# Stick-breaking / S5 hybrid block: order of the projection's passes by quarter, and two small steps on other engines

## The chip, the core and the metric

One core of a Trainium2 chip runs the whole program. TensorE multiplies 128x128 stationary tiles with streams of up to 512 columns, VectorE (DVE), ScalarE (ACT) and GpSimd (POOL) work on tiles of 128 partitions in SBUF, and only the first two also read PSUM, where TensorE writes. SyncE (SP) issues the DMAs. Every engine takes its instructions strictly in order. The metric is the device time of one execution in microseconds.

## What is computed

One residual block over 2048 frames of width 1024, float32. The part that the change touches is the combined projection (columns q, k, v, u, 512 each), the norm of each head of q and k, and the recurrence of the S5 half.

```python
xn = rmsnorm(h, norm1_g)
proj = xn @ w_in
q, k, v, u = jnp.split(proj, [512, 1024, 1536], axis=-1)
qh = rmsnorm(heads(q), q_norm_g)      # 8 heads of 64
kh = rmsnorm(heads(k), k_norm_g)
sb = stick_breaking_attention(qh, kh, heads(v))   # causal over 2048 frames
ssm = s5_glu(u, ...)                  # complex diagonal recurrence, GELU, half-GLU
h = h + concat(rmsnorm(sb), rmsnorm(ssm)) @ w_out
h = h + relu(rmsnorm(h) @ w1) ** 2 @ w2
```

## The kernel before

Products are made from float32 pairs: each operand is split into a rounded high part and the remainder (`hi` on ACT, `lo` on DVE), and `mm3` (lines 89 to 92) issues three matmuls, high by high, high by low and low by high.

**Projection** (`proj_stream`). The 2048 frames are four quarters Q = 3, 2, 1, 0 of four tiles j of 128 frames. The weight matrix is four groups gi of 512 columns: 0 is q, 1 is k, 2 is v, 3 is u. A job is one tile times one group: 8 row blocks by 3 matmuls, 24 matmuls. The list `jobs` holds 16 u jobs first, then for each quarter 4 jobs each of k, q and v, 64 in all. Before a group begins, its 8 blocks are loaded (`load_w`, 256 KB each, four buffers `wr`) and split (`split_w`: one 128x512 copy on ACT at line 157, one 128x512 instruction on DVE at line 158) during the job ahead; nine buffers hold split blocks. So each quarter loads and splits the k, q and v weights anew: 13 groups, 104 blocks.

**Evacuation** (`evac`). A v tile is split into `v` (lines 259 and 260). A q or k tile is copied to `p` (line 269), squared (271), reduced to 8 sums on DVE (273), divided by 64 and given its epsilon on DVE (274), raised to -1/2 and multiplied in on POOL (275, 276). Four jobs later `fin` transposes it on TensorE (284), splits it into `hi` and `lo` (288, 289; one buffer each) and stores both. A closing flag `kv{Q}` lets the attention of that quarter start.

**SSM** (`ssm_stream`). Runs between the projection's jobs in 16 chains. A chain rotates the projected input (`X`), scans it on DVE (line 769), rotates it back, and feeds TensorE (794) with the result. The rotation back makes `t1 = Xr*EC` on POOL and `t2`, in which the two halves of 64 partitions change places, by two DVE products of 64x512 (lines 775 and 776), and then subtracts.

**What sets the order.** `build` runs the projection with the SSM until the SSM ends, then with the attention until the projection ends, then the attention with the mixing of quarter 3 (`mix_stream`) and its MLP, and so on. From the instructions that come out of this interleaving a scheduler lays down each engine's final queue ahead of time; at run time nothing is reordered.

Of the kernel before, what the change touches and what calls it, by code (L numbers as in the profile page):

```python
# [11 lines left out]
ALU = mybir.AluOpType  # L12
ACTF = mybir.ActivationFunctionType
# [7 lines left out]
HD = 64  # L21
# [41 lines left out]
class Kern:  # L63
# [12 lines left out]
    def tt(self, eng, out, a, b, op):  # L76
        eng.tensor_tensor(out=out, in0=a, in1=b, op=op)  # L77
# [57 lines left out]
    def proj_stream(self):  # L135
        nc, A, S = self.nc, self.A, self.S
        NW = 4
        U, KV = 3, [1, 0, 2]
        jobs = [(("u",), Q, j, U) for Q in (3, 2, 1, 0) for j in range(4)]
        for Q in (3, 2, 1, 0):  # L140
            for gi in KV:
                jobs += [((Q, gi), Q, j, gi) for j in range(4)]
        group = {jb[0]: jb[3] for jb in jobs}
        first = jobs[0][0]
        xneed = [i for i, jb in enumerate(jobs) if jb[3] in (U, KV[0])]
        wt, wraw, xraw, xs = {}, {}, {}, {}

        def load_w(s, k):
# [72 lines left out]
        for i, (s, Q, j, gi) in enumerate(jobs):  # L221
            last = i + 1 == len(jobs) or jobs[i + 1][0] != s
            nxt = jobs[i + 1][0] if last and i + 1 < len(jobs) else None
            if i + 2 < len(jobs) and jobs[i + 1][0] == s and jobs[i + 2][0] != s:
                for k in range(NW):
                    load_w(jobs[i + 2][0], k)
            if i:
                feed_x(i)
            ps = self.ps_m.tile([128, 512], F32, tag="m", name="m")
            x, st = xs[Q, j], self.xst[:, 4 * Q + j, :]  # L230
            for k in range(8):
                w = wt[s, k]
                self.mm3(ps, x[:, 0, k, :], x[:, 1, k, :], w[:, 0, :], w[:, 1, :], k == 0, k == 7)
                if nxt:
                    split_w(nxt, k)
                    if k + NW < 8:
                        load_w(nxt, k + NW)
                if k == 0 and gi == U:
                    if i == 0:
                        feed_x(i)  # L240
                    stats(Q, j)
                if k == 1:
                    while pend and pend[0][0] <= i:
                        pend.pop(0)[1]()
                if k % 2 == 1:
                    yield 1.3
            self.evac(Q, gi, j, ps, st, i)
            if j == 3 and gi in (U, 2):
                pend.append((i + 1, lambda f=f"{'u' if gi == U else 'kv'}{Q}": self.flags.add(f)))
        for _, f in pend:  # L250
            f()
# [1 line left out]
    def evac(self, Q, gi, j, ps, st, i):  # L253
        nc, S = self.nc, self.S
# [12 lines left out]
        else:  # L267
            p = self.p_p.tile([128, 8, 64], F32, tag="p", name="p")
            nc.scalar.activation(out=p.rearrange("p h d -> p (h d)"), in_=ps, func=ACTF.Copy)
            sq = self.p_sq.tile([128, 8, 64], F32, tag="sq", name="sq")  # L270
            nc.scalar.activation(out=sq, in_=p, func=ACTF.Square)
            ss = self.p_tiny.tile([128, 16], F32, tag="ss", name="ss")
            nc.vector.tensor_reduce(out=ss[:, 0:8], in_=sq, axis=AX.X, op=ALU.add)
            self.ts(nc.vector, ss[:, 0:8], ss[:, 0:8], 1.0 / HD, ALU.mult, st[:, 2:3], ALU.add)
            self.tt(nc.gpsimd, ss[:, 8:16], ss[:, 0:8], self.mhalf[:, 0:8], ALU.pow)
            self.tt(nc.gpsimd, p, p, ss[:, 8:16].unsqueeze(2).to_broadcast([128, 8, 64]), ALU.mult)
            dst = S["qS"] if gi == 0 else S["kS"]
# [342 lines left out]
    def ssm_stream(self):  # L620
# [3 lines left out]
        tt, ts = self.tt, self.ts  # L624
# [110 lines left out]
        def chain(st, q, half):  # L735
# [35 lines left out]
                    data1=Xr[:, i, :], initial=0.0 if half else cy[:, i, 3:4], op0=ALU.mult, op1=ALU.add)  # L771
            t1, t2 = T([128, 4, 128]), T([128, 4, 128])
            tt(pool, t1, Xr, EC, ALU.mult)
            tt(dve, t2[0:64], Xr[64:128], E2[64:128], ALU.mult)
            tt(dve, t2[64:128], Xr[0:64], E2[0:64], ALU.mult)
            tt(pool, Xr, t1, t2, ALU.subtract)
            if half == 1:
                nc.vector.memset(X[:, :, 0:1], 0.0)
                nc.vector.tensor_copy(out=cy[:, :, 0:1], in_=X[:, :, 128:129])
# [762 lines left out]
```

## Time and profile before

| | us |
|---|---|
| median of 3 runs | 2605.67 (2601.1 to 2611.37) |
| the profiled execution | 2611.11 |
| its span, first to last instruction | 2609.4 |
| TensorE, matmul busy | 2471.2 (95%) |
| VectorE busy | 2069.8 (79%) |
| ScalarE busy | 1360.0 (52%) |
| GpSimd busy | 1023.4 (39%) |
| mean granted TensorE clock | 0.973 |

Busy shares over the whole span hide that the program has stages with different limits. By the records of lines 91 and 816, the projection's matmuls run to 564 us and the SSM's last result tile is written at 433 us; the attention begins between these two. The rows further below are read by stage.

### The profile page before, as it was taken

What the parts mean: (1) busy time and instruction counts of PE and PEld (TensorE: products, weight loads), DVE (VectorE), ACT (ScalarE), POOL (GpSimd) and SP (SyncE); (2) the same over time, 40 slices, a digit from 0 to 9 for tenths busy, and PEclk for the clock granted to TensorE, in tenths of its full rate; (3) what the DMA queues carried; (4) which work ended last, traced back from release to release, by engine and by line L of the source; (5) the groups of instructions that cost most, each with busy time, mean ns of one, the idle gap of its engine ahead of it and who ended that gap; (6) DMA issues with size and microseconds to landing.
All of it is one profiled execution on the core that took longest, in us unless ns stands there. A gap on an engine that the chain in (4) does not pass through costs nothing.

```text
span 2609.4 us, 36346 instructions
## 1 busy us (share of the span) xinstructions
PE 2471.2 (95%) x11984; PEld 2030.9 (78%) x11984; DVE 2069.8 (79%) x2990; ACT 1360.0 (52%) x2481; POOL 1023.4 (39%) x922
## 2 busy tenths in 40 slices
PE   8898888998889999999899899999999999989999
PEld 6776677876768888888777688888877888868887
DVE  7699997888998888899988976676687666676764
ACT  6444444765666666666566644444334444434443
POOL 5685856866775445444556421122100000020010
PEclk9999999998999999999989899999999999999999
DMA  8635457773433434333424234555444443594564
GB/s 290 200 115 171 130 158 213 212 222 117 136 113 122 126 116 120 105 109 99 144 83 152 85 113 160 178 178 182 141 149 151 161 141 138 181 322 156 192 223 164
DMA packets 290221, 408.88 MB, mean 157 GB/s; under 512 B 28016, under 2 KB 157808, under 8 KB 289520
## 3 DMA queue, kind: packets, MB, share of 16 engines
q1 hardware_dynamic: 290032, 406.55, 48.5%
q8 instruction: 95, 1.56, 0.2%
q14 instruction: 94, 0.77, 0.1%
HBM read 321.39 MB, written 83.89 MB: 155 GB/s over the span
## 4 chain that ended last, share of the span: by engine, by line
PE 63%; DVE 6%; DMA 3%; issue 2%; ACT 1%; POOL 0%; SPq 0%; DVEq 0%; ACTq 0%; POOLq 0%
PE m L90 10%; PE m L92 10%; PE m L91 10%; PE g L91 3%; PE g L92 3%; PE z L353 3%; PE g L90 3%; PE at L393 3%; PE o L413 2%; PE o L412 2%; PE fy L90 2%; PE fy L91 2%; PE fy L92 2%; DVE C L377 1%; DMA w<-in_w_dram 1%
## 5 line engine op out<-in xcount | busy, mean ns | idle before, releaser
L77 POOL TENSOR_TENSOR a<-a,C 128x512 f32<-128x512 f32 (+1 forms) x320 | 464.9, 1463 | 363.7 <-DVE C L377 134.2
L90 PE MATMUL m<-h,w 128*128 128x512 f32 (+1 forms) x992 | 359.2, 365 | 5.1 <-DVE h L77 2.7
L92 PE MATMUL m<-h,w 128*128 128x512 f32 (+1 forms) x992 | 357.8, 362 | 5.5 <-DVE w L77 5.4
L91 PE MATMUL m<-h,w 128*128 128x512 f32 (+1 forms) x992 | 357.7, 362 | 2.0 <-DVE h L77 1.9
L377 DVE TENSOR_TENSOR_SCAN C<-s,C,mz 128x513 f32<-128x513 f32 x192 | 273.4, 1440 | 16.7 <-ACT s L368 7.7
L368 ACT ACTIVATE s<-z 128x512 f32<-128x512 f32 (+1 forms) x320 | 172.2, 539 | 155.7 <-PE z L353 149.1
L397 ACT ACTIVATE hi<-at 128x512 fp32r<-128x512 f32 (+1 forms) x320 | 170.1, 541 | 140.5 <-PE at L393 123.8
L91 PE MATMUL m<-w,x 128*128 128x512 f32 x512 | 210.9, 412 | 14.7 <-DVE w L158 14.5
L77 DVE TENSOR_TENSOR lo<-at,hi 128x512 fp32r<-128x512 f32 (+1 forms) x320 | 185.7, 595 | 48.5 <-ACT hi L397 47.0
L90 PE MATMUL m<-w,x 128*128 128x512 f32 x512 | 208.9, 411 | 14.8 <-DVE v L260 6.1
L90 PEld LDWEIGHTS m<-h,w 128*128 128x128 f32 x992 | 189.3, 191 | 34.9 <-ACT w L909 3.0
L92 PEld LDWEIGHTS m<-h,w 128*128 128x128 f32 x992 | 189.4, 191 | 34.3 <-DVE w L77 7.6
L91 PEld LDWEIGHTS m<-h,w 128*128 128x128 f32 x992 | 189.8, 192 | 29.7 <-DVE h L77 4.0
L77 DVE TENSOR_TENSOR h<-h,m 128x512 f32<-128x512 f32 x256 | 170.1, 675 | 50.6 <-PE m L92 50.3
L92 PE MATMUL m<-w,x 128*128 128x512 f32 x512 | 208.3, 407 | 0.5 <-DVE x L77 0.5
L90 PE MATMUL m<-a,w 128*128 128x512 f32 x512 | 202.4, 396 | 2.2 <-DVE h L77 2.1
L91 PE MATMUL m<-a,w 128*128 128x512 f32 x512 | 200.4, 392 | 0.0
L92 PE MATMUL m<-a,w 128*128 128x512 f32 x512 | 200.1, 393 | 0.0
L77 DVE TENSOR_TENSOR w<-w,w 128x1024 fp32r<-128x1024 f32 x128 | 172.9, 1368 | 31.3 <-ACT w L1059 28.4
L77 POOL TENSOR_TENSOR s<-s,w 128x512 f32<-128x512 f32 x16 | 20.7, 1296 | 438.0 <-PE fx L92 376.3
L393 PE MATMUL at<-ident,a 128*128 128x128 f32 x1088 | 179.2, 281 | 4.6 <-POOL a L77 3.3
L91 PE MATMUL g<-hl 128*128 128x512 f32 x448 | 176.6, 394 | 1.9 <-DVE hl L77 1.3
(265 smaller groups left out, 6256.4 us busy)
## 6 DMA issues: line engine op xcount, KB each, us to landing
w<-in_w_dram SPq DMA_DIRECT2D x128, 512.0 KB, 3.7
w<-in_w_dram SPq DMA_DIRECT2D x128, 256.0 KB, 3.1
ar<-aS SPq DMA_DIRECT2D x112, 256.0 KB, 3.0
wr<-in_w_in_dram SPq DMA_DIRECT2D x104, 256.0 KB, 3.7
k<-kS SPq DMA_DIRECT2D x160, 128.0 KB, 3.2
v<-vS SPq DMA_DIRECT2D x80, 256.0 KB, 2.9
wr<-in_w_out_dram SPq DMA_DIRECT2D x40, 512.0 KB, 3.7
a<-in_w_dram SPq DMA_DIRECT2D x64, 256.0 KB, 3.1
```

What stands on the lines that cost most here:

```text
L77: eng.tensor_tensor(out=out, in0=a, in1=b, op=op)
L90: mm(ps, lh, rh, start=start, stop=False, skip_group_check=onto)
L91: mm(ps, lh, rl, start=False, stop=False, skip_group_check=onto)
L92: mm(ps, ll, rh, start=False, stop=stop, skip_group_check=onto)
L353: nc.tensor.matmul(z[:, i0:512], qt[g, h][m][:, u * 128:(u + 1) * 128], kt[b][:, i0:512], start=(m == 0), stop=(m == 1))
L368: nc.scalar.activation(out=s1[:, 1 + i0:513], in_=z[:, i0:512], func=ACTF.Sigmoid, scale=-0.125)
L377: nc.vector.tensor_tensor_scan(out=C[:, 0:513], data0=s1[:, 0:513], data1=self.mz[:, 128:641], initial=self.C[(n - 4) % 6][:, 512:513], op ...
L393: nc.tensor.transpose(at[:, u * 128:(u + 1) * 128], at_a[b, u][:, kb * 128:(kb + 1) * 128], self.ident)
L397: nc.scalar.activation(out=hi[:, :n], in_=at[:, :n], func=ACTF.Copy)
L412: nc.tensor.matmul(o[:, :n], vt[b][:, kb, :], hi[:, :n], start=first, stop=False)
L413: nc.tensor.matmul(o[:, :n], vt[b][:, kb, :], lo[:, :n], start=False, stop=last)
```

## The change

Three things. The order of the passes now differs by quarter (k, q, v for quarters 3 and 1; v, q, k for quarters 2 and 0), and a weight group's name counts up only where the group differs from the job ahead. So v serves quarters 3 and 2 in a row, k serves 2 and 1, and v serves 1 and 0: 10 groups, 80 blocks. Quarters 2 and 0 close with k, so their flag follows k. The division by 64 goes into the square's scale on ACT, and the remaining addition goes from DVE to POOL. In the rotation back, ACT copies the two halves into each other's place, one DVE product of 128x512 follows, and POOL adds instead of subtracting.

```diff
--- before.py
+++ after.py
@@ -135,14 +135,18 @@
     def proj_stream(self):
         nc, A, S = self.nc, self.A, self.S
         NW = 4
-        U, KV = 3, [1, 0, 2]
+        U = 3
+        order = {3: (1, 0, 2), 2: (2, 0, 1), 1: (1, 0, 2), 0: (2, 0, 1)}
         jobs = [(("u",), Q, j, U) for Q in (3, 2, 1, 0) for j in range(4)]
+        turn = 0
         for Q in (3, 2, 1, 0):
-            for gi in KV:
-                jobs += [((Q, gi), Q, j, gi) for j in range(4)]
+            for gi in order[Q]:
+                if jobs[-1][3] != gi:
+                    turn += 1
+                jobs += [((turn, gi), Q, j, gi) for j in range(4)]
         group = {jb[0]: jb[3] for jb in jobs}
         first = jobs[0][0]
-        xneed = [i for i, jb in enumerate(jobs) if jb[3] in (U, KV[0])]
+        xneed = [i for i, jb in enumerate(jobs) if jb[3] == U or jb[3] == order[jb[1]][0]]
         wt, wraw, xraw, xs = {}, {}, {}, {}
 
         def load_w(s, k):
@@ -245,7 +249,7 @@
                 if k % 2 == 1:
                     yield 1.3
             self.evac(Q, gi, j, ps, st, i)
-            if j == 3 and gi in (U, 2):
+            if j == 3 and (gi == U or gi == order[Q][2]):
                 pend.append((i + 1, lambda f=f"{'u' if gi == U else 'kv'}{Q}": self.flags.add(f)))
         for _, f in pend:
             f()
@@ -268,10 +272,10 @@
             p = self.p_p.tile([128, 8, 64], F32, tag="p", name="p")
             nc.scalar.activation(out=p.rearrange("p h d -> p (h d)"), in_=ps, func=ACTF.Copy)
             sq = self.p_sq.tile([128, 8, 64], F32, tag="sq", name="sq")
-            nc.scalar.activation(out=sq, in_=p, func=ACTF.Square)
+            nc.scalar.activation(out=sq, in_=p, func=ACTF.Square, scale=HD ** -0.5)
             ss = self.p_tiny.tile([128, 16], F32, tag="ss", name="ss")
             nc.vector.tensor_reduce(out=ss[:, 0:8], in_=sq, axis=AX.X, op=ALU.add)
-            self.ts(nc.vector, ss[:, 0:8], ss[:, 0:8], 1.0 / HD, ALU.mult, st[:, 2:3], ALU.add)
+            self.ts(nc.gpsimd, ss[:, 0:8], ss[:, 0:8], st[:, 2:3], ALU.add)
             self.tt(nc.gpsimd, ss[:, 8:16], ss[:, 0:8], self.mhalf[:, 0:8], ALU.pow)
             self.tt(nc.gpsimd, p, p, ss[:, 8:16].unsqueeze(2).to_broadcast([128, 8, 64]), ALU.mult)
             dst = S["qS"] if gi == 0 else S["kS"]
@@ -771,9 +775,10 @@
                     data1=Xr[:, i, :], initial=0.0 if half else cy[:, i, 3:4], op0=ALU.mult, op1=ALU.add)
             t1, t2 = T([128, 4, 128]), T([128, 4, 128])
             tt(pool, t1, Xr, EC, ALU.mult)
-            tt(dve, t2[0:64], Xr[64:128], E2[64:128], ALU.mult)
-            tt(dve, t2[64:128], Xr[0:64], E2[0:64], ALU.mult)
-            tt(pool, Xr, t1, t2, ALU.subtract)
+            nc.scalar.activation(out=t2[0:64], in_=Xr[64:128], func=ACTF.Copy)
+            nc.scalar.activation(out=t2[64:128], in_=Xr[0:64], func=ACTF.Copy)
+            tt(dve, t2, t2, E2, ALU.mult)
+            tt(pool, Xr, t1, t2, ALU.add)
             if half == 1:
                 nc.vector.memset(X[:, :, 0:1], 0.0)
                 nc.vector.tensor_copy(out=cy[:, :, 0:1], in_=X[:, :, 128:129])
```

On DVE, where quarter 3's v jobs end and the next group begins (before: k of quarter 2), the queue of before has the splits `w` between the SSM's rotations (`t`, `X`, `EC`, `E2`), its tables (`tt`, `CP`) and the evacuations (`v`, `lo`):

```order
L158 SCALAR_TENSOR_TENSOR w_2410<-wr_2318,sm_69,w_2410 128x512
L158 SCALAR_TENSOR_TENSOR w_2451<-wr_2320,sm_69,w_2451 128x512
L77 TENSOR_TENSOR tt_2297<-e2_752,e1_751 128x512
L289 SCALAR_TENSOR_TENSOR lo_2421<-m_2415,sm_69,hi_2420 128x512
L158 SCALAR_TENSOR_TENSOR w_2459<-wr_2322,sm_69,w_2459 128x512
L158 SCALAR_TENSOR_TENSOR w_2477<-wr_2405,sm_69,w_2477 128x512
L769 SCALAR_TENSOR_TENSOR X_2225<-rho8_535,X_2225 128x128 x4
L260 SCALAR_TENSOR_TENSOR v_2525<-m_2398,xst_111,v_2525 128x8x64
L77 TENSOR_TENSOR x_2720<-xr_2532,x_2720 128x1024
L77 TENSOR_TENSOR tt_2308<-PI_457,Q2_2274 128x512
L77 TENSOR_TENSOR CP_2290<-PIr_459,bc_2269 128x576
L77 TENSOR_TENSOR t_2354<-X_2225,E2_1918 64x512 x2
```

The queue of after at the same v jobs:

```order
L264 SCALAR_TENSOR_TENSOR v_2388<-m_2322,xst_111,v_2388 128x8x64
L773 SCALAR_TENSOR_TENSOR X_2231<-rho8_535,X_2231 128x128 x4
L77 TENSOR_TENSOR x_2578<-xr_2395,x_2578 128x1024
L293 SCALAR_TENSOR_TENSOR lo_2410<-m_2404,sm_69,hi_2409 128x512
L77 TENSOR_TENSOR t_2376<-m_2371,EC_1921 128x512
L77 TENSOR_TENSOR t_2377<-m_2371,E2_1922 64x512 x2
L77 TENSOR_TENSOR t_2352<-t_2352,E2_1922 128x512
L77 TENSOR_TENSOR tt_2314<-PI_457,Q2_2280 128x512
L264 SCALAR_TENSOR_TENSOR v_2493<-m_2397,xst_111,v_2493 128x8x64
L77 TENSOR_TENSOR tt_2313<-tt_2313,tt_2314 128x512
L77 TENSOR_TENSOR x_2679<-xr_2500,x_2679 128x1024
```

The splits are gone from this place, and `t<-X,E2 64x512 x2` has become one `t<-t,E2 128x512`.

On ACT, later in the SSM, around the thirteenth loading of a u tile (`u2<-ur`), before:

```order
L745 ACTIVATE u2_3075<-ur_3072 128x512
L269 ACTIVATE p_3231<-m_3151 128x512
L157 ACTIVATE w_3254<-wr_3143,sm_69 128x512
L271 ACTIVATE sq_3233<-p_3231 128x512
L157 ACTIVATE w_3287<-wr_3145,sm_69 128x512
L750 ACTIVATE uT_3074<-m_3077 128x512
L157 ACTIVATE w_3295<-wr_3147,sm_69 128x512
L288 ACTIVATE hi_3264<-m_3259,sm_69 128x512
L157 ACTIVATE w_3308<-wr_3249,sm_69 128x512
L157 ACTIVATE w_3314<-wr_3257,sm_69 128x512
```

and after:

```order
L778 ACTIVATE t_2804<-X_2655 64x512
L779 ACTIVATE t_2804<-X_2655 64x512
L749 ACTIVATE u2_3004<-ur_3001 128x512
L161 ACTIVATE w_3165<-wr_3070,sm_69 128x512
L273 ACTIVATE p_2979<-m_2919 128x512
L275 ACTIVATE sq_2981<-p_2979 128x512
L778 ACTIVATE t_2949<-X_2827 64x512
L779 ACTIVATE t_2949<-X_2827 64x512
L754 ACTIVATE uT_3003<-m_3006 128x512
L273 ACTIVATE p_3061<-m_2988 128x512
```

The pairs `t<-X 64x512` are new, and here fewer weight copies `w` stand between the evacuations (`p`, `sq`).

On PE, at the last matmul of the projection, before (`o`, `at` and `z` are the attention's):

```order
L92 MATMUL m_6959<-w_6550,x_5744 128x512
L412 MATMUL o_5261<-hi_5225,v_4927 128x512
L413 MATMUL o_5261<-lo_5226,v_4927 128x512
L412 MATMUL o_5261<-hi_5257,v_4927 128x384
L413 MATMUL o_5261<-lo_5258,v_4927 128x384
L393 MATMUL at_5303<-ident_71,a_5004 128x128
L353 MATMUL z_5356<-k_5241,qh_5106 128x512
L353 MATMUL z_5356<-k_5241,ql_5107 128x512
L353 MATMUL z_5401<-k_5241,qh_5106 128x512
L353 MATMUL z_5401<-k_5241,ql_5107 128x512
```

and, behind the last projection matmul, after:

```order
L288 MATMUL m_6918<-ident_71,p_6535 128x128
L288 MATMUL m_6929<-ident_71,p_6668 128x128 x4
L288 MATMUL m_6940<-ident_71,p_6797 128x128 x4
L357 MATMUL z_5479<-k_5300,qh_5294 128x128
L357 MATMUL z_5479<-k_5300,ql_5295 128x128
L397 MATMUL at_5458<-ident_71,a_5192 128x128
L397 MATMUL at_5458<-ident_71,a_5216 128x128
L416 MATMUL o_5440<-hi_5404,v_5121 128x512
L417 MATMUL o_5440<-lo_5405,v_5121 128x512
L416 MATMUL o_5440<-hi_5436,v_5121 128x384
```

In the queue of before the last transposes `m<-ident,p` stand ahead of the projection's last matmul; now all 16 of the last four k tiles stand behind it, among the attention's matmuls.

## Rows read from the trace of the kernel before

**Rows 1.** Busy us of each engine (instructions) by stage, TensorE's clock, DMA share, GB/s.
```profile
core 0: us, PE busy (x) PEld busy (x) DVE busy (x) ACT busy (x) POOL busy (x), PEclk, DMA share, GB/s
...
90.00:435.00 345.00, 295.87 (x1541) 240.71 (x1542) 308.21 (x439) 156.02 (x257) 232.00 (x195) 0.95 0.51 152
435.00:565.00 130.00, 126.64 (x648) 105.64 (x648) 109.56 (x153) 89.78 (x194) 103.93 (x103) 0.97 0.75 219
565.00:640.00 75.00, 59.70 (x257) 45.84 (x256) 65.83 (x74) 45.37 (x94) 45.62 (x34) 0.84 0.49 152
640.00:1500.00 860.00, 819.16 (x3986) 669.32 (x3985) 775.87 (x909) 531.73 (x1005) 467.83 (x356) 0.96 0.37 117
1500.00:2609.00 1109.00, 1089.56 (x5234) 906.02 (x5232) 745.86 (x1160) 483.46 (x839) 117.06 (x95) 1.00 0.51 172
```

**Rows 2.** Waits of the matmul engine, 90 to 435 us: us in total, times, longest.
```profile
PE m L91 <- DVE w L158: 14.5, 12, 3.2
PE m L715 <- issue: 7.7, 1, 7.7
PE m L715 <- DVE tt L77: 7.4, 3, 2.9
PE m L284 <- DVE lo L289: 7.0, 6, 2.4
PE m L90 <- DVE v L260: 6.1, 2, 4.3
```

**Rows 3.** Busy us by engine, columns as in rows 1, three shorter stretches.
```profile
400.00:450.00 50.00, 44.49 (x207) 35.36 (x206) 36.76 (x49) 27.40 (x49) 34.53 (x35) 0.92 0.82 230
450.00:500.00 50.00, 50.00 (x256) 42.23 (x255) 41.55 (x60) 37.05 (x80) 37.24 (x39) 0.98 0.72 218
500.00:550.00 50.00, 49.92 (x264) 41.74 (x263) 44.87 (x65) 36.12 (x81) 45.97 (x44) 1.00 0.70 204
```

**Rows 4.** DVE groups, 90 to 435 us: count | busy, mean ns | idle before, releaser.
```profile
L158 DVE SCALAR_TENSOR_TENSOR w<-wr,sm,w 128x512 fp32r<-128x512 f32 x70 | 68.2, 997 | 4.1 <-ACT w L157 3.8
L77 DVE TENSOR_TENSOR t<-X,E 64x512 f32<-64x512 f32 x32 | 31.9, 996 | 0.7
L74 DVE TENSOR_SCALAR ss<-ss,xst 128x8 f32<-128x8 f32 x23 | 16.0, 696 | 0.3
L77 DVE TENSOR_TENSOR tt<-e,e 128x512 f32<-128x512 f32 x15 | 15.5, 1030 | 6.4 <-POOL EC L77 6.4
```

**Rows 5.** The same operations' ns min/median/max, by tile.
```profile
L74 DVE TENSOR_SCALAR ss<-ss,xst x32: 203/270/4672, 126.4 to 535.4; 128x8 f32<-128x8 f32 x32
...
L77 DVE TENSOR_TENSOR t<-m,E x32: 683/689/694, 128.4 to 392.5; 64x512 f32<-64x512 f32 x32
L77 DVE TENSOR_TENSOR t<-X,E x32: 684/724/1742, 132.7 to 402.6; 64x512 f32<-64x512 f32 x32
...
L158 DVE SCALAR_TENSOR_TENSOR w<-wr,sm,w x70: 721/746/2381, 111.4 to 434.4; 128x512 fp32r<-128x512 f32 x70
```

**Rows 6.** POOL groups, small tiles, 0 to 420 us, columns as in rows 4.
```profile
L72 POOL TENSOR_SCALAR phs<-phs 128x32 f32<-128x32 f32 x10 | 5.1, 513 | 0.0
L77 POOL TENSOR_TENSOR ss<-ss,mhalf 128x8 f32<-128x8 f32 x22 | 41.8, 1902 | 26.9 <-DVE ss L74 26.3
```

**Rows 7.** Timeline of the matmul engine where quarter 2 begins: start, us, [idle before].
```profile
233.00 0.50 PE L91 MATMUL m<-w,x 128*128 128x512 f32 x1 [1.78 <-DVE w L158]
```

**Rows 8.** ACT groups, 90 to 435 us, columns as in rows 4.
```profile
L157 ACT ACTIVATE w<-wr,sm 128x512 fp32r<-128x512 f32 x70 | 48.3, 718 | 54.6 <-DMA wr<-in_w_in_dram 42.9 <-PE m L284 6.3 <-PE m L794 4.7
L745 ACT ACTIVATE u<-ur 128x512 f32<-128x512 f32 x15 | 9.4, 626 | 17.1 <-DMA ur<-uS 17.1
```

**Rows 9.** Waits of ACT, 90 to 435 us, columns as in rows 2.
```profile
ACT w L157 <- DMA wr<-in_w_in_dram: 42.9, 18, 7.5
```

**Rows 10.** Waits, 0 to 565 us, columns as in rows 2.
```profile
ACT hi L288 <- DMA kS<-hi: 7.0, 2, 5.3
```

**Rows 11.** Timeline of the matmul engine where the mixing begins, columns as in rows 7.
```profile
574.41 0.50 PE L90 MATMUL m<-h,w 128*128 128x512 f32 x1 [1.81 <-ACT w L909]
579.41 0.80 PE L92 MATMUL m<-h,w 128*128 128x512 f32 x1 [2.97 <-DVE w L77]
```

## The prediction

> **What bounds the kernel now.** I read the stages first [rows 1]. From 1500 us on TensorE is busy 98% of the time and none of the change's work is there. From 435 to 565 us, projection with attention, it is busy 126.6 of 130 us. The stage that the change works in, projection with SSM from 90 to 435 us, is different: TensorE is busy 295.9 of 345 us, so 49.1 us idle, while DVE is busy 308.2, which is 89%, its highest share of any long stage but 640 to 1500. ACT (45%) and POOL (67%) have room. Second, who ends TensorE's idle time there [rows 2]: 14.5 us end with a weight split of line 158, 7.4 with a table `tt`, 7.0 with `lo`, 6.1 with `v`, all on DVE; 7.7 us is one start-up pause. So in this stage DVE sets the pace and TensorE waits. Third, what a DVE share does to TensorE [rows 3]: with DVE at 41.6 and 44.9 of 50 us TensorE had no idle time; from 400 to 450 us, at 36.8, it still idled 5.5 us, so chains through several engines cost something by themselves.
>
> **The change part by part.** The sum is made against the profiled execution, 2611.1 us (span 2609.4), which is 5.4 above the median 2605.67; I carry the difference over to the median.
>
> *Weight splits.* 24 of 104 loads, ACT copies and DVE splits vanish, at the three places where the group stays: the starts of quarters 2, 1 and 0. The first two lie in the stage, 16 blocks. At 0.997 us [rows 4] that is 16.0 us of DVE; at the undisturbed median 0.746 [rows 5], 11.9. On the way TensorE's direct waits at such a place go, as the 1.78 us at 233 us [rows 7]. ACT loses 16 x 0.718 = 11.5 us [rows 8]. The loads lie beside other traffic (DMA share 0.51 [rows 1]); I cost them at nothing.
>
> *Halves.* 32 products of 64x512 go, 31.9 us [rows 4]. In their place 16 of 128x512 come; the row nearest in form, both inputs in SBUF and 128x512, is `tt<-e,e` at 1.030 us [rows 4], so 16.5 us and a saving of 15.4. Undisturbed they would cost 0.689 [rows 5], a saving of 20.9. ACT gains 32 copies; the nearest SBUF-to-SBUF copy took 0.626 us [rows 8], so 20.0 us. POOL's subtraction becomes an addition, nothing.
>
> *The norm's mean.* 23 DVE instructions on 128x8 leave the stage: 23 x 0.696 = 16.0 us [rows 4]. Their median is only 0.270, the longest 4.672 [rows 5]: a few long ones carry the mean. If whatever blocked those few blocks the next DVE instruction instead, only 23 x 0.270 = 6.2 us are gained. POOL gets one small instruction each; the nearest on POOL took 0.513 us, against 1.902 for the power that follows it there [rows 6], so 23 x 0.513 = 11.8 us on an engine with 113 us idle, off the path. The factor moved into the square costs nothing on ACT, since the square is there already.
>
> The blocking can be seen: the half product with one input in PSUM took 683 to 694 ns every time, the one with both in SBUF 684 to 1742 [rows 5]. The Trainium skill, "SBUF — State Buffer", section "SBUF: two separate sides", says that a DVE instruction in a two-port mode, or with two SBUF inputs, shares a port pair with GpSimd under an exclusive lock held for a whole instruction; the two rows agree. By that rule the delay of 16.0 - 6.2 us would partly pass on to the next DVE instruction with two SBUF inputs, and the term would be nearer 6.2.
>
> DVE in the stage: 16.0 + 15.4 + 16.0 = 47.4 us less, between 11.9 + 15.4 + 6.2 = 33.5 and 16.0 + 20.9 + 16.0 = 52.9. It falls from 308.2 to about 261.
>
> *How much of it TensorE gets.* Not all: as DVE gets room, TensorE becomes the limit. If DVE kept its share of 0.893, the stage would shrink to 261 / 0.893 = 292 us, which TensorE can't follow, since it has 295.9 us to do; without any idle time but the start-up pause it would be 295.9 + 7.7 = 304, a gain of 41. If only the waits at the vanished places went, 2 of the 8.75 group changes that the stage's 70 splits [rows 4] make up, the gain would be 14.5 x 2 / 8.75 = 3. In 450 to 550 us TensorE ran dense with DVE at 86.4 of 100 us [rows 3]; here chains tie three engines, and I take a share of 0.83: 261 / 0.83 = 314, a gain of **31**, with 3 and 41 as ends. The upper end may be too low: weight loads were busy 240.7 of 345 us here and 105.6 of 130 in the next stage [rows 1]; at that pace the same loads take 296 us, a gain of 49. The Trainium skill, "Perfetto Trace Analysis", section "Identifying the Most-Contended Engine", calls weight-load busy time a fair measure of TensorE's headroom and matmul busy time a bad one; by it the end would be 49 and not 41.
>
> The clock is in this already: the 345 us had it granted at 0.95 of its upper level, 2.4 GHz [rows 1]. If fewer pauses come, fewer stretches at the lower level, 1.2 GHz, may follow; I take nothing extra for it.
>
> *435 to 565 us.* One group change fewer, but only 3.4 us idle there: 0. In TensorE's queue the SSM's last matmul stands behind 42.7 jobs of projection matmuls, before behind 45.8: three jobs move from the first stage into this one, and as much of the attention ahead of the projection's end. TensorE's work stays the same: 0.
>
> *The projection's end.* Quarter 0 now ends with k, so four `fin` pieces follow the last matmul. Before, v ended it and the transposes were hidden under v's matmuls; that cover is gone. ACT's `hi` has one buffer: each piece waits until the store of the one ahead has landed; such waits came twice, 7.0 us in total and 5.3 at longest [rows 10]. Behind a waiting `hi` on ACT stand the attention's sigmoids and the weight copies of the mixing, and behind SP's stores stand the mixing's loads; TensorE waits for such a copy there already, 1.81 and 2.97 us [rows 11]. Three such waits could cost 3 x 3.5 = 10.5; the queue puts attention matmuls between the four pieces, which hide most. I take **4**, from 0 to 12.
>
> Sum: -31 + 4 = **-27**: 2611.1 becomes 2584, and the median 2605.67 - 27 = **2579**. What is redealt later, when everything behind 435 us stands in another order, I can't sign: 640 to 1500 us has 40.8 us of TensorE idle time [rows 1], and a third of it either way is 13.
>
> **Rivals.** *No change.* TensorE's idle time in the stage is then not DVE's load but chain latency and a fixed order: DVE gets idle, TensorE still waits. For it: the 5.5 us idle at DVE 36.8 of 50 [rows 3]. Against: most waits end with single long DVE queues [rows 2]. Gain 3, tail 4: 2607. That the change does not do what it says belongs here; the queues hold 80 loads instead of 104, and the moved instructions are where it says, so it gets almost nothing.
>
> *Slower: ACT becomes the chain's slow link.* The copies stand in ACT's queue behind weight copies that wait for their load: 42.9 us of ACT's idle time in the stage over 18 waits, 2.4 each [rows 9]. A chain would then take 2 x 0.626 + 1.030 for 2 x 0.996, 0.3 longer, and 2.4 with the wait: 2.7 x 16 chains = 43 us if TensorE's next product of each chain waits for all of it. Then -31 + 4 + 43 = +16: **2622**. It decides from about 1.7 us per chain, 27 / 16. Against it: in the queue of after most of the 16 pairs stand behind evacuations and not right behind a weight copy, and two chains are always under way.
>
> *More than forecast.* All idle time goes, and the later redealing helps: -49 + 0 to -13 gives 2544 to 2557.
>
> **How the numbers follow.** Forecast mechanism, 2560 to 2592: 0.62. More: 0.12. No change, 2593 to 2618: 0.16. Slower, 2619 and up: 0.10. The range leaves out half of "more" and, at the other end, the slower case and part of no change, 2 in 10 in all: 2552 to 2606. A measurement of this kernel can tell about 0.5%, 13 us, from no change. Faster by more: 0.74; within: 0.16; slower: 0.10.
>
> **What would show it.** Right: up to the SSM's last result tile, DVE's busy time falls by 34 to 53 us beside what the three moved jobs carry, TensorE's idle time falls from 49 to about 20 us, and that tile is written some 31 us earlier and, for the three jobs, some 15 to 25 more. The 128x512 product takes 0.69 to 1.1 us; the small POOL addition 0.25 to 0.6. The tail shows as `hi` waiting for a store near the projection's end, under 12 us. Wrong: the stage as long as before with DVE idle (no change), or `t<-t,E` waiting for ACT and TensorE's line 799 matmuls waiting for POOL's `X` (slower), or more than 15 us of new TensorE pauses where the mixing begins.

## The result, and the profile after

The changed kernel took 2584.01 us (median of 4 runs, 2580.71 to 2586.45), the kernel before 2606.84 beside it (2601.1 to 2611.37): ratio 0.9916, 95% interval 0.9899 to 0.9932, so 0.84% faster. The profiled execution took 2586.45 us, its span 2584.7, against 2611.1 and 2609.4. The forecast was 2579 in 2552 to 2606. Its sum was nearly right, and two of its steps, what leaves DVE and what TensorE gets of it, were wrong in ways that largely cancelled; most of what follows is about those.

First the stages of the kernel after, columns as in rows 1, with the stage ends moved to about where the same work ends.

```profile
90.00:395.00 305.00, 267.02 (x1438) 218.16 (x1439) 262.61 (x368) 153.12 (x254) 223.63 (x205) 0.97 0.50 147
395.00:540.00 145.00, 144.97 (x757) 122.23 (x756) 117.54 (x156) 100.46 (x213) 115.20 (x119) 1.00 0.71 200
540.00:640.00 100.00, 84.53 (x396) 68.51 (x395) 87.80 (x106) 65.17 (x137) 69.15 (x62) 0.88 0.54 163
640.00:1475.00 835.00, 790.02 (x3860) 644.52 (x3859) 766.20 (x881) 514.69 (x970) 441.80 (x339) 0.97 0.36 115
1475.00:2584.00 1109.00, 1088.40 (x5216) 904.53 (x5214) 735.41 (x1151) 477.47 (x823) 105.12 (x89) 0.99 0.51 172
```

Behind 395 us little changed: TensorE has no idle time up to 540, 15.5 us of 100 where the mixing begins (15.3 of 75 before), and 45.0 in the next stage (40.8 before). The last result tile `yT`, with which the stage of the forecast (projection with SSM) ends, started at 396.6 us, before at 432.7: 36.1 us earlier, where the prediction had some 31 and 15 to 25 more for the projection jobs that now follow it. To compare nearly equal work I cut both kernels at the start of their 2000th matmul, which lies a little behind the SSM's end. First before, then after:

```profile
0.00:467.90 467.90, 405.77 (x2001) 327.90 (x2002) 399.68 (x731) 231.49 (x393) 309.45 (x356) 0.95 0.59 184
```

```profile
0.00:440.80 440.80, 391.77 (x2001) 318.63 (x2002) 367.32 (x677) 241.49 (x418) 325.58 (x391) 0.98 0.60 184
90.00:396.60 306.60, 268.62 (x1445) 219.49 (x1446) 264.21 (x370) 153.99 (x255) 225.15 (x206) 0.97 0.50 147
```

The first 2000 matmuls took 27.1 us less. Counted by matmuls the gain was 2.9 us at the 1000th, 16.6 at the 1500th, 27.1 at the 2000th, between 24.7 and 33.7 at every 500th from there on, and 24.7 at the last: it all arises in the forecast's stage. DVE's busy time fell by 32.4 us, TensorE's idle time (the stretch less its busy time) from 62.1 to 49.0, and its busy time by 14.0, with the clock granted at 0.98 in place of 0.95.

The 2000 matmuls aren't quite the same work: in after 1230 of them are the projection's, before 1259, and the attention's, many of them shorter, make up the number; they stream 737,536 columns in place of 745,344. Cut where 745,344 columns have been streamed, after stands at 444.7 us against 467.9: the gain is 23.2 us, made of 13.1 us less idle and 10.1 us less busy time of TensorE, and DVE's busy time is 28.4 us less.

Who ends TensorE's idle time in the stage after (90 to 395 us, columns as in rows 2; lines behind 158 have moved by 4, those behind 776 by 5):

```profile
PE m L719 <- DVE tt L77: 12.2, 5, 4.1
PE m L91 <- DVE w L162: 9.4, 5, 3.4
PE m L719 <- issue: 7.8, 1, 7.8
PE m L288 <- DVE lo L293: 5.6, 5, 1.5
PE m L799 <- POOL X L77: 3.4, 4, 1.2
PE m L90 <- DVE v L264: 1.4, 1, 1.4
```

The splits end 9.4 us where they ended 14.5 [rows 2], `v` 1.4 for 6.1, but the tables `tt` 12.2 for 7.4: one wait shrank, another grew, and DVE is still behind most of them. POOL's `X` has joined the list. The DVE groups of the stage after (90 to 396.6 us, columns as in rows 4):

```profile
L162 DVE SCALAR_TENSOR_TENSOR w<-wr,sm,w 128x512 fp32r<-128x512 f32 x48 | 52.5, 1119 | 1.8 <-ACT w L161 1.8
L773 DVE TENSOR_TENSOR_SCAN X<-rho,X 128x128 f32<-128x128 f32 x32 | 22.1, 750 | 5.2 <-POOL X L77 5.2
L77 DVE TENSOR_TENSOR tt<-e,e 128x512 f32<-128x512 f32 x14 | 17.0, 1213 | 2.6 <-POOL EC L77 2.6
L77 DVE TENSOR_TENSOR t<-t,E 128x512 f32<-128x512 f32 x16 | 13.2, 822 | 5.8 <-ACT t L779 5.5
```

The splits fell from 70 to 48 (16 as reckoned; the other 6 are the share of the three jobs that now follow the stage), but each takes 1119 ns for 997 [rows 4], and a table `tt` 1213 for 1030. The scan, which the change doesn't touch, took 505 ns before, as this row of 90 to 435 us shows, and takes 750 now:

```profile
L769 DVE TENSOR_TENSOR_SCAN X<-rho,X 128x128 f32<-128x128 f32 x32 | 14.3, 505 | 0.7 <-POOL X L77 0.7
```

The moved pieces, ns min/median/max over the whole projection (columns as in rows 5), first the mean on POOL and the power behind it, then the new product; and under them the weight copies and the swaps' copies on ACT (columns as in rows 4):

```profile
L72 POOL TENSOR_SCALAR ss<-ss,xst x32: 309/323/1402, 125.1 to 546.6; 128x8 f32<-128x8 f32 x32
L77 POOL TENSOR_TENSOR ss<-ss,mhalf x32: 1657/1668/2477, 125.5 to 547.0; 128x8 f32<-128x8 f32 x32
...
L77 DVE TENSOR_TENSOR t<-t,E x16: 676/692/1414, 136.2 to 368.9; 128x512 f32<-128x512 f32 x16
...
L161 ACT ACTIVATE w<-wr,sm 128x512 fp32r<-128x512 f32 x48 | 32.9, 716 | 16.8 <-DMA wr<-in_w_in_dram 16.1 <-PE m L92 0.7
L778 ACT ACTIVATE t<-X 64x512 f32<-64x512 f32 x16 | 10.1, 630 | 38.6 <-DVE X L773 38.5
```

### The profile page after: what moved, and what is told of

Its sections match the earlier page's. It is cut to its first block, busy times and chain, and to the rows that moved or that the text cites. A ratio compares the mean times of both kernels' runs of the same rounds, so it can differ in the third digit from the quotient of the medians.

```text
span 2584.7 us, 36210 instructions
## 1 busy us (share of the span) xinstructions
PE 2453.9 (95%) x11984; PEld 2020.2 (78%) x11984; DVE 2034.8 (79%) x2918; ACT 1365.8 (53%) x2489; POOL 1014.7 (39%) x954
## 4 chain that ended last, share of the span: by engine, by line
PE 72%; DVE 13%; POOL 4%; issue 4%; DMA 4%; ACT 3%; SPq 0%; DVEq 0%; ACTq 0%; POOLq 0%
PE m L92 13%; PE m L90 13%; PE m L91 13%; PE at L397 4%; PE z L357 4%; PE g L91 3%; PE g L92 3%; PE g L90 3%; PE o L417 2%; PE o L416 2%; DVE C L381 2%; PE fy L90 2%; PE fy L91 2%; PE fy L92 2%; PE fx L90 1%
## 5 line engine op out<-in xcount | busy, mean ns | idle before, releaser
L77 POOL TENSOR_TENSOR a<-a,C 128x512 f32<-128x512 f32 (+2 forms) x320 | 450.0, 1415 | 336.1 <-DVE C L381 150.5
L91 PE MATMUL m<-h,w 128*128 128x512 f32 (+1 forms) x992 | 357.4, 361 | 10.9 <-DVE h L77 10.7
L91 PE MATMUL m<-w,x 128*128 128x512 f32 x512 | 205.6, 402 | 9.4 <-DVE w L162 9.4
L90 PE MATMUL m<-w,x 128*128 128x512 f32 x512 | 206.8, 406 | 8.0 <-ACT w L161 5.5
L92 PE MATMUL m<-w,x 128*128 128x512 f32 x512 | 205.1, 401 | 0.5 <-DVE x L77 0.5
L77 POOL TENSOR_TENSOR s<-s,w 128x512 f32<-128x512 f32 x16 | 20.7, 1294 | 463.1 <-ACT v L1225 395.3
L373 ACT ACTIVATE a<-z 128x512 f32<-128x512 f32 (+1 forms) x320 | 169.4, 542 | 17.2 <-PE at L397 16.7
```

The source lines that it names most:

```text
L90: mm(ps, lh, rh, start=start, stop=False, skip_group_check=onto)
L91: mm(ps, lh, rl, start=False, stop=False, skip_group_check=onto)
L92: mm(ps, ll, rh, start=False, stop=stop, skip_group_check=onto)
L373: nc.scalar.activation(out=a[:, i0:512], in_=z[:, i0:512], func=ACTF.Sigmoid, scale=0.125)
```

## The experiments

I call the parts O (the order of the passes), H (half swaps on ACT, one product in place of two) and M (the norm's mean on POOL). My theory: the stage takes the time that DVE takes, at about the exchange rate of the forecast. The rivals: ACT as the slow link of the SSM's chain, POOL as the engine that sets the pace, and a fixed order of chains in which DVE's load matters little.

**The parts alone.** O alone:

```diff
-        U, KV = 3, [1, 0, 2]
...
+        order = {3: (1, 0, 2), 2: (2, 0, 1), 1: (1, 0, 2), 0: (2, 0, 1)}
...
+                if jobs[-1][3] != gi:
+                    turn += 1
+                jobs += [((turn, gi), Q, j, gi) for j in range(4)]
...
```

> The kernel before with the new order of passes alone (80 weight blocks, k last in quarters 2 and 0). DVE-pace theory: 16 splits of 1.0 us leave the stage with the SSM, a third of the removed DVE time, so about a third to a half of the whole gain: 8 to 11 us faster, minus a few us at the projection's end. Rival 'only the group changes matter' (a change of group stalls TensorE, the other two parts are hidden): 20 to 25 us faster, all of it here. Rival 'tail': k at the end costs more than it showed: 0 or slower.

Measured: 2596.11 us, ratio 0.9954 (0.9941 to 0.9966). H alone:

```diff
-            tt(dve, t2[0:64], Xr[64:128], E2[64:128], ALU.mult)
-            tt(dve, t2[64:128], Xr[0:64], E2[0:64], ALU.mult)
-            tt(pool, Xr, t1, t2, ALU.subtract)
+            nc.scalar.activation(out=t2[0:64], in_=Xr[64:128], func=ACTF.Copy)
+            nc.scalar.activation(out=t2[64:128], in_=Xr[0:64], func=ACTF.Copy)
+            tt(dve, t2, t2, E2, ALU.mult)
+            tt(pool, Xr, t1, t2, ALU.add)
```

> The kernel before with the rotation back through two ACT copies and one DVE product alone. DVE-pace theory: 18.7 us of DVE go from the stage with the SSM, 9 to 12 us faster. Rival 'only the group changes matter': within 4 us of before. Rival 'ACT link': with all 104 weight copies still in ACT's queue, many of them waiting for loads, the copies of the halves wait behind them: 0 to 15 us slower.

Measured: 2585.48, ratio 0.9912 (0.9898 to 0.9926). M alone:

```diff
-            nc.scalar.activation(out=sq, in_=p, func=ACTF.Square)
+            nc.scalar.activation(out=sq, in_=p, func=ACTF.Square, scale=HD ** -0.5)
...
-            self.ts(nc.vector, ss[:, 0:8], ss[:, 0:8], 1.0 / HD, ALU.mult, st[:, 2:3], ALU.add)
+            self.ts(nc.gpsimd, ss[:, 0:8], ss[:, 0:8], st[:, 2:3], ALU.add)
```

> The kernel before with the norm's addition on POOL and the factor in the square alone. DVE-pace theory with the full mean duration: 16.0 us of DVE leave the stage, 8 to 10 us faster. With the blocked time passed on to the next DVE instruction: only 23 x 0.27 = 6.2 us leave, 2 to 4 us faster, and the mean duration of the splits, scans and table products on DVE rises. Rival 'only the group changes matter': within 3 us of before.

Measured: 2598.87, ratio 0.9961 (0.9949 to 0.9974). Each part alone is a gain, and H alone is as fast as all three. By the ratios O brings 12.0 us, H 22.9 and M 10.2. H is twice what was expected of it (9 to 12), and M agrees with the price by its full mean (8 to 10), not with the lower one (2 to 4). ACT as the slow link falls here: H alone has all 104 weight copies on ACT and the 32 swap copies as well, and is the best of the three.

**The parts in twos, and all three again.** The edits are those above put together: H and M, then the change as it is, then O and H, and O and M.

> The changed kernel with the old order of passes, so halves and mean together. DVE-pace theory: the sum of the two single runs, 12 to 20 us faster than before. Rival 'only the group changes matter': within 5 us of before.

> The changed kernel itself once more, beside its variants on one chip. Expected 0.991 to 0.993 of before, and, if the profile of after is typical, about 20 us at the lower clock within the first 2000 matmuls (44 in the profile of before) and about 49 us of TensorE idle time there (62 before). If the low-clock time comes out near 40 again, the part of the gain that I now read as clock was a chance of one execution.

> The changed kernel with the norm's addition back on DVE. Theory 'the moved addition only hands POOL's blocking on to other DVE instructions': as fast as the changed kernel or up to 8 us faster, with splits and scans on DVE shorter on average than in the changed kernel (1.12 and 0.75 us there). Theory 'each part takes DVE time away and adds': 6 to 10 us slower than the changed kernel.

> The changed kernel with the rotation back as before (two DVE products, a subtraction). Alone the halves gave 23 us. If they carry the change, this is 8 to 15 us slower than the changed kernel; if any two parts are enough because another limit comes next, within 6 us of it.

Measured: H and M 2592.73, ratio 0.9946 (0.9932 to 0.9959); all three 2585.72, 0.9919 (0.9906 to 0.9933); O and H 2583.21, 0.9906 (0.9893 to 0.9920); O and M 2599.07, 0.9968 (0.9955 to 0.9980). So the gains don't add: O 0.46%, H 0.88% and M 0.39% would make 1.7%, and the three bring 0.84. M, a gain by itself, is none beside another part: it goes with a loss from H to H and M, where the intervals don't overlap; the other two pairs point the same way, with intervals that do. Each edit also lays all queues down anew, and no run separates a part's own work from that.

The table puts the profiles of all kernels side by side, each up to its 2000th matmul (us); its last column is the time at which 745,344 columns have been streamed, and so compares equal amounts of TensorE's work. "Undisturbed" takes every DVE instruction at the tenth percentile of its own kind (same operation, same tiles); "blocked" is what its instructions took beyond that. Both are sums of durations, and instructions overlap a little, so they add to more than DVE's busy time. Worked out with kinds by operation, tiles and shape, the undisturbed sums come out 1 to 4 us lower and the blocked ones within 3 of the table's.

| kernel | ratio | time | DVE busy | time less DVE busy | undisturbed | blocked | TensorE idle | time at equal columns |
|---|---|---|---|---|---|---|---|---|
| before | 1 | 467.9 | 399.7 | 68.2 | 365.2 | 78.6 | 62.1 | 467.9 |
| O | 0.9954 | 452.2 | 383.1 | 69.1 | 352.6 | 72.4 | 51.0 | 455.1 |
| H | 0.9912 | 446.3 | 375.4 | 70.9 | 353.8 | 70.1 | 45.5 | 446.1 |
| M | 0.9961 | 457.8 | 389.7 | 68.1 | 358.8 | 72.6 | 55.2 | 457.5 |
| H, M | 0.9946 | 449.3 | 374.7 | 74.6 | 347.5 | 73.3 | 51.0 | 451.2 |
| O, M | 0.9968 | 453.2 | 381.8 | 71.4 | 351.0 | 73.5 | 54.0 | 456.5 |
| O, H | 0.9906 | 436.9 | 372.4 | 64.5 | 343.1 | 75.1 | 41.9 | 440.3 |
| after | 0.9916 | 440.8 | 367.3 | 73.5 | 338.2 | 71.8 | 49.0 | 444.7 |
| after, again | 0.9919 | 442.6 | 366.8 | 75.8 | 339.4 | 71.4 | 47.3 | 446.6 |
| first rotation too | 0.9940 | 447.3 | 360.4 | 86.9 | 326.5 | 78.8 | 48.8 | 450.6 |
| O, H, no power | 0.9942 | 444.5 | 375.5 | 69.0 | 344.5 | 73.9 | 47.8 | 450.6 |
| O, H, more POOL | 0.9954 | 445.1 | 370.1 | 75.1 | 336.0 | 76.2 | 45.2 | 443.9 |
| O, H, more DVE | 0.9970 | 458.1 | 391.5 | 66.6 | 360.1 | 82.2 | 60.0 | 461.0 |
| O, H, v last | 0.9890 | 440.5 | 372.9 | 67.6 | 341.6 | 76.4 | 47.5 | 443.8 |

How far one profile of each can be trusted is seen in two rows. Up to this point O, H and "O, H, v last" run the same instructions in the same order on TensorE, DVE, ACT and POOL, and yet (columns as in rows 1):

```profile
0.00:436.90 436.90, 394.99 (x2000) 323.96 (x2001) 372.39 (x700) 241.25 (x416) 311.76 (x364) 0.96 0.59 185
0.00:440.50 440.50, 392.96 (x2001) 322.11 (x2002) 372.93 (x701) 242.22 (x418) 312.02 (x364) 0.96 0.59 183
```

The times differ by 3.6 us and TensorE's idle times by 5.6, so differences of that size between two rows show nothing.

Two columns hardly move. The time is DVE's busy time plus 64 to 76 us in every kernel but one. And the blocked time stays between 70 and 82 us, whatever is taken from DVE. In these terms the parts miss their sum by the blocked time: undisturbed, O, H and M take 12.6, 11.4 and 6.4 us from DVE, 30.4 in sum, and together 27.0, which is nearly all. But each alone also takes 6.2, 8.5 and 6.0 us of blocked time along, 20.7 in sum, and together they take 6.8. The single parts share the one profile of before; that they don't add doesn't rest on it, for the ratios, from 4 runs or more of each, say the same.

**More DVE work.** On O and H, two products more per chain, 32 of 128x512, read by nobody:

```diff
             tt(dve, t2, t2, E2, ALU.mult)
+            for _ in range(2):
+                tt(dve, self.xtra, t2, E2, ALU.mult)
```

> Order and halves, with two products of 128x512 more on DVE in each of the 16 chains, behind the chain's own work and read by nobody: some 32 x 0.8 = 26 us of DVE. DVE-limit theory: 12 to 26 us slower than 2583. POOL-limit theory: 0 to 8 us slower.

Measured: 2597.71, ratio 0.9970 (0.9958 to 0.9982). The DVE groups from 90 to 410 us, columns as in rows 4:

```profile
L77 DVE TENSOR_TENSOR xtra<-t,E 128x512 f32<-128x512 f32 x32 | 37.8, 1183 | 0.2
L162 DVE SCALAR_TENSOR_TENSOR w<-wr,sm,w 128x512 fp32r<-128x512 f32 x47 | 39.7, 895 | 2.6 <-ACT w L161 2.6
```

The new products took 37.8 us, but the splits got shorter, 895 ns each for 1065 in O and H, and DVE's busy time rose by 19.1 us, its undisturbed time by 17.0. The 2000th matmul came 21.2 us later, and by the ratios the kernel took 0.64% or 16.7 us longer. DVE's load is paid for about one for one, and the price of an instruction in the trace is not its price: the 32 products are worth 17 to 21 us and not 38.

**The power gone from POOL.** On O and H, the power on POOL left out:

```diff
-            self.ts(nc.vector, ss[:, 0:8], ss[:, 0:8], 1.0 / HD, ALU.mult, st[:, 2:3], ALU.add)
-            self.tt(nc.gpsimd, ss[:, 8:16], ss[:, 0:8], self.mhalf[:, 0:8], ALU.pow)
+            self.ts(nc.vector, ss[:, 8:16], ss[:, 0:8], 1.0 / HD, ALU.mult, st[:, 2:3], ALU.add)
```

> Order and halves as in the fastest variant so far, with the power of line 275 on POOL left out (the heads are scaled by the mean square itself): 32 POOL instructions of 1.7 us, 54 us, go; DVE keeps its work. This leaves out a part of the computation. Theory 'behind the halves POOL and the chain through it are the next limit': 10 to 25 us faster than that variant (2583), all of it before the SSM's end. Theory 'DVE is still the limit': within 5 us of it.

Measured: 2591.3, ratio 0.9942 (0.9930 to 0.9954), and the row up to the 2000th matmul, columns as in rows 1:

```profile
0.00:444.50 444.50, 396.75 (x2001) 325.28 (x2002) 375.54 (x707) 242.38 (x424) 278.37 (x348) 0.95 0.59 181
```

POOL is busy 33.4 us less than with O and H (311.8), and the time is no shorter but 7.6 us longer, with DVE's blocked time as before, 73.9 for 75.1; at equal columns it is 10.3 us longer, and over the whole kernel 9.4 by the ratios. Neither theory had that: one said 10 to 25 us faster, the other within 5. So POOL's load doesn't set the pace. Why it got longer I can't say; what follows POOL's powers starts at other times, and the queues meet differently.

**More POOL work.** On O and H, one product more per chain on POOL:

```diff
             tt(pool, Xr, t1, t2, ALU.add)
+            tt(pool, self.xtra, t1, t2, ALU.add)
```

> Order and halves, with one product of 128x512 more on POOL in each of the 16 chains, behind the chain's own work and read by nobody: some 16 x 1.4 = 22 us of POOL. POOL-limit theory: 8 to 20 us slower than 2583. DVE-limit theory: the extra reads block two-input DVE instructions now and then, 0 to 5 us slower.

Measured: 2594.19, ratio 0.9954 (0.9942 to 0.9966). The group on POOL, 0 to 420 us:

```profile
L77 POOL TENSOR_TENSOR xtra<-t 128x512 f32<-128x512 f32 x16 | 25.2, 1576 | 0.0
```

25.2 us of POOL work cost 8.2 us up to the 2000th matmul and, by the ratios, 12.5 in all. That lies where the theory of POOL's pace had it (8 to 20) and not where that of DVE's had it (0 to 5). But at equal columns the stage is only 3.6 us longer, POOL's busy time rose by 8.8 us and not by 25.2, and blocked time by 1.1 only. Since work taken from POOL also cost 7.6 us, differences of some 8 us between such variants can't be put down to POOL's load.

**The first rotation through ACT too.** On the changed kernel, the same exchange for the rotation ahead of the scans, which reads PSUM:

```diff
-            tt(dve, t2[0:64], P[64:128], E2[64:128], ALU.mult)
-            tt(dve, t2[64:128], P[0:64], E2[0:64], ALU.mult)
-            tt(pool, Xr, t1, t2, ALU.add)
+            nc.scalar.activation(out=t2[0:64], in_=P[64:128], func=ACTF.Copy)
+            nc.scalar.activation(out=t2[64:128], in_=P[0:64], func=ACTF.Copy)
+            tt(dve, t2, t2, E2, ALU.mult)
+            tt(pool, Xr, t1, t2, ALU.subtract)
```

> The changed kernel with the chain's first rotation done in the same way: ACT copies the two halves out of PSUM crosswise, one DVE product of 128x512 in place of two of 64x512 (0.69 us each, never blocked), POOL subtracts. DVE-pace theory: 32 x 0.69 - 16 x 0.82 = 9 us less on DVE, 3 to 6 us faster than the changed kernel. Rival: products with one input in PSUM are never blocked, the new one is, and ACT gets 32 more copies (20 us): no gain or up to 8 us slower.

Measured: 2589.80, ratio 0.9940 (0.9921 to 0.9958). Up to its 2000th matmul:

```profile
0.00:447.30 447.30, 398.47 (x2001) 326.22 (x2002) 360.35 (x661) 261.57 (x451) 329.91 (x392) 0.96 0.59 183
```

DVE's undisturbed time fell by another 12 us against after, its busy time by 6 to 7, and the stage got 4.7 to 6.5 us longer; over the whole kernel the interval overlaps that of after. This is the one kernel in which the time less DVE's busy time left its band, with 86.9. That DVE no longer sets the pace alone here is a reading; which engine of the chain took over I did not separate.

**v last again.** On O and H, quarter 0 as k, q, v: one change of the weight group more, and the projection ends with v as before.

```diff
-        order = {3: (1, 0, 2), 2: (2, 0, 1), 1: (1, 0, 2), 0: (2, 0, 1)}
+        order = {3: (1, 0, 2), 2: (2, 0, 1), 1: (1, 0, 2), 0: (1, 0, 2)}
```

> Order and halves, but quarter 0 in the order k, q, v: v closes the projection again and the closing k transposes go, for one group of 8 weight blocks more, loaded and split between 435 and 540 us where TensorE has next to no idle time. If the closing k costs what I put on it (0 to 12 us, 4 taken): 2 to 6 us faster than 2583. If it costs nothing: same, or 1 to 4 us slower.

Measured: 2576.64, ratio 0.9890 (0.9875 to 0.9904), the lowest time of all. Its interval just touches that of the change, and overlaps that of O and H, from which it differs by this edit alone (0.16%, 4.2 us). What it takes away is seen in O and H. There TensorE, where the closing k pieces are transposed, waited for `p` (its timeline: start, us, [idle before]):

```profile
554.64 1.12 PE L288 MATMUL m<-ident,p 128*128 128x128 f32 x4 [7.24 <-POOL p L77]
```

and on POOL two selects of the attention's stood ahead of `p` for 6.83 us:

```profile
545.14 1.64 POOL L77 TENSOR_TENSOR ss<-ss,mhalf 128x8 f32<-128x8 f32 x1
546.74 6.83 POOL L378 TENSOR_SCALAR_AFFINE_SELECT a<-a 128x128 f32<-128x128 f32 x2
553.55 1.04 POOL L77 TENSOR_TENSOR p<-p,ss 128x512 f32<-128x512 f32 x1
```

In after two such selects took 0.54 us, at 549.21, and TensorE's wait for `p` was 0.26; what held the two in O and H for so long stays open. The kernel with O alone has the same pause of 7.24 us, at 570.69 us, O and M one of 7.6. The five kernels that end with v don't have it.

## Why the prediction was right, and where it was not

**What bounds the stage.** Right: DVE. Up to the 2000th matmul the time follows DVE's busy time in both directions, 27.1 less for 32.4 less in the change, 21.2 more for 19.1 more with the added products. "No change" falls with that, and POOL as the pace falls with the run without powers.

**The DVE terms: the step that failed.** The prediction took 47.4 us from DVE, at least 33.5; it lost 32.4. Alone, O took 16.6 us of busy time (forecast 16.0), M 10.0 (6.2 to 16.0) and H 24.3 (15.4 to 20.9), 50.9 in sum. What failed is adding three terms priced at mean durations. O and H together took 27.3 us, of 31.4 forecast; M beside them took 5.1 more (372.4 to 367.3), of 16.0 forecast, and brought no time. A mean holds time in which the instruction is blocked. With one part alone some of that time went too; with all three little of it went. Priced at undisturbed durations [rows 5] the sum would have been 11.9 for the splits, 6.2 for the mean, and 32 x 0.689 - 16 x 0.689 = 11.0 for the halves: 29.1, against 23.2 in time at equal columns and 27.1 at the 2000th matmul. (The 27.0 undisturbed of the table is no check on this, as it is made of the same durations.) In time at equal columns this price comes nearer than the mean's in five of the seven kernels that hold one, two or three parts. It fails most for H, which brought 21.8 us for 11.0; why H brings so much stays open.

Where the blocked time goes can be read from one place in each trace. Before, DVE's mean (first fence) against POOL (second), start and us:

```profile
261.11 0.69 DVE L273 TENSOR_REDUCE ss<-sq 128x8 f32<-128x512 f32 x1
261.83 4.67 DVE L74 TENSOR_SCALAR ss<-ss,xst 128x8 f32<-128x8 f32 x1
266.41 0.68 DVE L77 TENSOR_TENSOR tt<-e,e 128x512 f32<-128x512 f32 x1
```

```profile
261.93 1.28 POOL L77 TENSOR_TENSOR EC<-tt 128x512 f32<-128x512 f32 x1
263.18 1.03 POOL L77 TENSOR_TENSOR p<-p,ss 128x512 f32<-128x512 f32 x1
264.18 1.27 POOL L77 TENSOR_TENSOR X<-t 128x512 f32<-128x512 f32 x1
265.43 1.04 POOL L77 TENSOR_TENSOR tt<-e,e 128x512 f32<-128x512 f32 x1
```

The small DVE instruction, 0.270 us by its median [rows 5], lasts 4.67 and ends as POOL's fourth long instruction in a row ends. After, the mean is gone from DVE. At another place four scans in a row are long beside POOL's:

```profile
250.53 4.18 DVE L773 TENSOR_TENSOR_SCAN X<-rho,X 128x128 f32<-128x128 f32 x4 [2.20 <-POOL X L77]
```

```profile
250.45 1.28 POOL L77 TENSOR_TENSOR E<-tt 128x512 f32<-128x512 f32 x1
251.81 1.06 POOL L77 TENSOR_TENSOR tt<-PR,Q 128x512 f32<-128x512 f32 x1
253.05 1.38 POOL L77 TENSOR_TENSOR tt<-PRr,bc 128x576 f32<-128x576 f32 x1 [0.18 <-DMA M<-tt]
```

They take 4.18 us beside three POOL instructions of 1.06 to 1.38; by the median of before they need 4 x 0.40. Over the stretch up to the 2000th matmul it is the same. Before, 129 DVE instructions were more than 0.05 us over their undisturbed time, 74.9 us in all. POOL is busy beside every one of them, and beside 372 of the other 602. The mean has 10.9 of the 74.9 and the scans `X<-rho,X` 3.4; after it is 68.1 us in 119 instructions, the mean none, these scans 11.3. Put down to the POOL instruction that overlaps longest, POOL's power has 0.7 us of it before and 0.2 after, which fits that its removal freed nothing; `X<-t` has most, 18.1 us before and 26.1 after. That POOL's instructions hold DVE's up is thus read from who overlaps whom, before and after; that the blocked time stays at 70 to 82 us is measured in 14 profiles, and why it stays there is not settled.

The Trainium skill, "SBUF — State Buffer", section "SBUF: two separate sides", has a DVE instruction in a two-port mode, or one with two SBUF inputs against a POOL instruction that reads SBUF, and that POOL instruction shut each other out by an exclusive lock, which whichever starts first holds for its whole instruction. The places above agree, but for two things: 4.67 us is four instructions of POOL's, not one, and POOL's power, whose inputs lie in SBUF too, held up next to nothing. By that rule the mean's term was to be nearer 6.2 than 16.0, and M took 10.0 us of busy time alone and 5.1 beside O and H.

**The exchange rate.** 31 us out of 47.4 was 0.65; measured are 27.1 out of 32.4, or 0.84 (23.2 out of 28.4 at equal columns, 0.82). Too much taken from DVE and too little given to TensorE partly cancelled: 31 was forecast for the stage. The forecast let DVE's share of the stage fall from 0.893 to 0.83; it fell to 0.862 (264.21 of 306.60). The limit behind that step, TensorE's work and 7.7 us of start-up, was not reached: TensorE's idle time fell by 13.1 us and not from 49 to 20, 38.0 remain from 90 to 396.6 us (306.6 less 268.6). The rest of the gain came where nothing was reckoned: TensorE was busy 14.0 us less, of which 10.1 are left at equal columns.

**The clock.** "Nothing extra" was wrong in size. In the profile's clock records TensorE stood at the lower level, 1.2 GHz, for 44.4 us before the 2000th matmul in the kernel before, and for 20.5 and 34.1 us in the two profiles of after. The time hardly differs between those two, 440.8 and 442.6: idle time and busy time share the gain as 13.1 and 14.0 in one, 14.8 and 10.5 in the other. That fits a time set by DVE, whichever way TensorE spends it. The Trainium skill in its second place, "Perfetto Trace Analysis", section "Identifying the Most-Contended Engine", would have allowed a gain of 49; the weight loads were busy 327.9 us before and 318.6 after for the first 2000, and the gain of 23 to 27 stayed below both ends, so no run here tests the rule.

**The tail.** Forecast 4 us, from 0 to 12, for ending with k. From the 2000th matmul to the start of the last the kernels that end with v took 2126.4 to 2137.2 us (mean of five 2133.3), those that end with k 2134.7 to 2140.1 (mean of nine 2138.5): about 5 us, within groups that spread as much. From equal columns on it is 3.0, and without "v last" 0.6, so the size can't be told from nothing. The mechanism was not seen at work: in after one `hi` waits for a store behind 400 us, 1.0 us at 426 us, and none near the projection's end. In O and in O and H one does wait there, 2.3 and 2.0 us, but the pause is TensorE's for POOL's `p`. What the rest of the kernel, forecast at 0, gave or took is no more than the 24.7 to 33.7 of the count by matmuls.

**Slower through ACT.** Fell, as said. The new product waited for ACT 5.5 us, in 3 waits, and the weight copies' waits for their loads shrank from 42.9 us [rows 9] to 16.1. What came instead is the wait for POOL's `X` that the prediction named as a sign: in after, 0 to 600 us, columns as in rows 2,

```profile
DVE X L773 <- POOL X L77: 5.2, 2, 3.0
PE m L799 <- POOL X L77: 3.4, 4, 1.2
```

and such waits of DVE's scans are 4.0 to 5.2 us in all kernels with M, 0 to 1.2 in those with neither M nor added POOL work. They come with M, whose addition on POOL takes 0.323 us by its median and up to 1.402. I did not separate them from the redealing of the queues, so how much of M's missing gain they are stays open.

## What to carry to other kernels

Where one engine sets a stage's pace, price what you take from it by the undisturbed durations (the lower percentiles of each kind) as well as by the means, and don't count on the difference: here blocked time stayed nearly the same in sum, though one part alone brought more than its undisturbed price. Don't add the gains of parts that were each priced, or measured, alone; run the combination and each part left out, since here one part of three was worth nothing beside the others. Compare at equal work: the first 2000 matmuls of two queues differed by 1% in columns, and the gain by 3.9 us. And after a reordering look at what closes each loop: the last pass had its cover in the pass behind it, and the kernel that gave one saved group change back to have it again had the lowest time, though not clear of the noise.

## What the runs showed of the hardware

- One small DVE instruction (128x8, 0.270 us by its median) stood for 4.67 us beside four POOL instructions in a row of 1.03 to 1.28 us, so a stop can outlast one instruction of the other engine.
- A scan from SBUF gets longer too: 128x128, 0.400 us by its median before, 0.505 in the mean before and 0.750 after, up to 1.49.
- POOL's power on 128x8 (1.668 us by its median) is long, and DVE loses next to nothing by it: without it DVE's blocked time was 73.9 us for 75.1.
- Up to the 2000th matmul TensorE was at the lower clock level for 20.5 us in one profile of the changed kernel and 34.1 in another, with 1.8 us between their times.
- Two kernels whose engines run the same instructions in the same order up to the 2000th matmul reached it at 436.9 and 440.5 us, with 41.9 and 47.5 us of TensorE idle time.
